# Moving the gate products of a state space mixer two steps forward, and giving the work shared by two engines to VectorE alone around three norms

## The chip, the cores and the metric

The kernel runs on one NeuronCore of one Trainium2 chip. The core has a matrix engine (TensorE, PE in the profile, with PEld for its weight loads), three engines for everything else (VectorE is DVE, ScalarE is ACT, GpSimd is POOL) and a queue that issues transfers (SyncE, SP). Each engine runs its own instructions in the order in which the program lists them, and waits where an operand isn't ready. The metric is the device time of one execution in microseconds (us).

## The reference, cut to what matters

Two layers follow one another on a sequence of 512 tokens with 1024 features. All products are in float32 accuracy.

- First layer: `h = rmsnorm(x)`, a gated delta-rule mixer and a latent attention on `h`, merged by two gates, then `x = x + merged @ w_out`.
- Feed-forward: `h = rmsnorm(x)`, `u = conv(h @ w_up)`, `x = x + (silu(gate_f) * up_f) @ w_down`, and a last `rmsnorm(x)`.
- Second layer: `h = rmsnorm_2(x)` and `proj = h @ w_in`, which is cut into `xbc` (1280 columns), `dt` (16), `z_ssd`, `sc_h`, `sc_b`, `sc_c` and `z_sc` (1024 each).
  - State space part: `xbc` goes through a convolution and SiLU; a chunked scan gives `y_ssd` (16 heads of 64); `yz = y_ssd * silu(z_ssd)`; each of two groups of 512 features is normed by itself.
  - Short convolution: `y_sc = sc_b * conv(sc_c * sc_h) * silu(z_sc)`.
  - `mix = concat(y_ssd, y_sc) @ w_out`, `x = x + rmsnorm(mix)`, and the result is `x + sigmoid(x @ w_ple_gate) * (p @ w_ple_proj)`.

Four norms run over all 1024 features of the residual stream or of `mix`. The change touches the three that stand between two stages of products: the one after `w_out` of the first layer (below: the first norm), the pair after `w_down`, which the kernel computes as one (the second norm), and the one over `mix` (the third norm).

## The kernel before, in words

Activations lie transposed: 128 features on the partitions, the 512 tokens along the row. A product of a 128x128 weight block with a 128x512 tile is three matmuls, because each operand is split into a high part `hi` (rounded to fp32r) and a remainder `lo`: hi by hi, hi by lo and lo by hi. An output tile over 1024 features is 8 blocks, so 24 matmuls of 512 columns. The whole kernel has 1872 such triples.

**Weights.** `order()` (L111) lists the outputs in the order of their products; `pack_weights` lays the blocks out in that order in chunks of 8, and `load_chunk` (L534) streams them. For each chunk `t_chunk` (L557) makes `hi` on ScalarE and `lo` on VectorE or GpSimd; there are two buffers for the raw chunk and three for the split ones.

**Shared work.** `idle` (L431) decides between GpSimd and VectorE for the work that either can do: `lo` of a weight chunk (L570), the multiplication by the norm's scale in `normalised` (L868, tile `xn`), the sum of the squares of some norms (L687), a step of the triangular solve (L1030) and the addition `mix + xr` after the third norm (L1937). It takes the engine that would be free earlier by the program's own clocks, with a bias.

**Planner.** The program is written by generators that are driven by a table of modelled clocks (`Timeline`, L250; `drive`, L467). A generator yields what it waits for; the one whose operand is ready first by the model goes on, the products of the main line when no other is earlier. So the order on each engine's queue is fixed when the program is built, and any change in an engine's modelled load rearranges what comes after it.

**Norms.** `t_rs` (L857) sums the squares as the residual tiles come, transposes and reduces them (`cs`, `ms_a`), takes the inverse root on 128x4 tiles (`rsqrt`, L636: some twelve tiny VectorE instructions), spreads it over the partitions (`bcast`, L665: tile `rs`), and `normalised` multiplies each tile by it and splits it. So that TensorE need not wait, the first three pairs of outputs of the next stage run on the tiles that aren't normed, and are multiplied by `rs` afterwards; `unfold` (L1526) then switches to the normed ones. `t_final` (L1597) does the same for the second norm. The third, `t_post` (L1886) with `t_x2` (L1931), is covered by the eight small `pp` products (`p @ w_ple_proj`), after which the `pg` products need the first normed tile (tile `mix`).

**Second layer.** `block2` (L1890) runs the `xbc` products, and then for each m of 8: the gate product `zs` (its SiLU goes to `zd[m]`), the products `sh`, `sc` (for m of 3 and more; those of the first three ran before), `sb` and `sz`. After the `zs` product of m the generator `t_ssd` of m is spawned (L1779): it loads two rows of 256 KB and two of 128 KB, builds the decay matrices on VectorE, ScalarE and GpSimd, has TensorE compute `y`, adds the skip and multiplies by the gate. At most two of these are at work at a time (`LIMIT`, L222). `t_group` (L1824) norms tiles 0 to 3 and 4 to 7 and splits them into `ym`. The `mix` products follow; each reads 16 activation tiles, `ym` 0 to 7 first and the tiles of the short convolution, 8 to 15, after them. Also in the second layer, `t_dt` (L1643) works out `dt`: a small product, a copy `dtz` on VectorE, and four transposes of it on TensorE, which stand in the middle of the `xbc` products.

Of the kernel before, what the change touches and what calls it, by code (L numbers as in the profile page):

```python
# [37 lines left out]
PAIR_FFN = 3  # L38
FOLD_FFN = 3
FOLD_B2 = 3  # L40
XBC = [8, 9, 0, 1, 2, 3, 4, 5, 6, 7]


# [55 lines left out]
def qr_of(h):  # L99

    return [("qr", 0)] if h == 0 else [("qr", h // 2 + 1)] if h % 2 and h < 7 else []


def order():


    one = lambda keys: [[k] for k in keys]
    kq = lambda h: one([("k", h), ("q", h)])
    vg = lambda h: one([("v", h), ("ga", h)])
    o = [START] + one([("ckv", 0), ("ckv", 1)]) + [FIRST] + one([("q", 1), ("k", 2), ("q", 2)])  # L110
    for item in GDN_ORDER:  # L111
        if item[0] == "kq":
            o += kq(item[1])
        elif item[0] == "vg":
            o += vg(item[1])
        elif item[0] == "low":
            pass
        elif item[0] == "wv":
            o += one([("wv", kt, h) for kt in range(2) for h in range(4 * item[1], 4 * item[1] + 4)])
        elif item[0] in ("bra", "brb", "ya"):  # L120
            o.append([item])
        else:
            h = item[1]
            o += one(qr_of(h) + [("kn", h), ("qn", h)])
    o += [[("yb", 0), ("yb", 1)]] + one([("yb", m) for m in range(2, 8)])
    o += one([("out", m) for m in range(8)])
    pair = lambda f: [("fg", f), ("fu", f)]
    for f in range(12):
        o += [pair(f)] if f < PAIR_FFN else one(pair(f))
    o += one([("fd", 0, m) for m in range(8)])  # L130
    o += one([x for f in range(12, 22) for x in pair(f)])
    o += one([("fd", 1, m) for m in range(8)])
    xbc = [("xbc", m) for m in XBC]
    o += [[("sh", m), ("sc", m)] for m in range(FOLD_B2)] + [["dt2"]] + one(xbc)
    for m in range(8):
        o += one([("zs", m)] + ([("sh", m), ("sc", m)] if m >= FOLD_B2 else []) + [("sb", m), ("sz", m)])
    o += one([("mix", m) for m in range(8)])
    o += one([("pp", m) for m in range(8)])
    o += [[("pg", 0), ("pg", 1), ("pg", 2)]] + one([("pg", m) for m in range(3, 8)])
    return o  # L140
# [92 lines left out]
class Engine:  # L233


    def __init__(self, tl, name, eng):
        self.tl, self.name, self.eng = tl, name, eng
# [157 lines left out]
class Emit:  # L395
# [5 lines left out]
    def __init__(self, ctx, tc, a, out):  # L401
        self.tc, self.a, self.out = tc, a, out
        self.nc = self.tl = Timeline(tc.nc)
        E = ctx.enter_context
        self.const = E(tc.tile_pool(name="const", bufs=1))
        self.wp = E(tc.tile_pool(name="wp", bufs=1))
        self.gp = E(tc.tile_pool(name="gp", bufs=1))
        self.sm = E(tc.tile_pool(name="sm", bufs=1))
        self.ps = E(tc.tile_pool(name="ps", bufs=1, space=PSUM))
        self.dr = E(tc.tile_pool(name="dr", bufs=1, space=DRAM))  # L410
        self.n = 0
        self.nmm = 0
        self.mms = []
        self.held = None
        self.specs = weight_specs()
        self.order = order()
        self.opos = 0
        self.bpos = 0
        self.blocks = {}
        self.his = {}  # L420
        self.nchunk = a["wstream"].shape[0]
        self.loaded = 0
        self.tasks = []
        self.waiting = {}
        self.nspawn = 0
        self.flags = set()
        self.live = []
        self.hold = 1 << 30
        self.using = None

    def idle(self, pool, dve, bias=0):  # L431

        now = self.tl.clk["PE"]
        t = lambda e: max(self.tl.clk[e], now)
        if t("DVE") - now > BACKLOG:
            return self.nc.vector
        return self.nc.gpsimd if t("POOL") + pool <= t("DVE") + dve + bias else self.nc.vector
# [918 lines left out]
    def block1(self):  # L1356
# [155 lines left out]
        def t_out(m, x, ps):  # L1512
            yield [x, ps]
            nc.vector.tensor_tensor(x, x, ps, ALU.add)
            self.xr[m] = x
            self.xh[m] = yield from self.split(x, self.par("norm_ffn_g", m))
# [3 lines left out]
        for m in range(8):  # L1520
            x = self.g(name="xr")
            nc.sync.dma_start(x, self.a["xT"][m])
            ps = yield from self.linear(("out", m), mg)
            self.spawn(t_out(m, x, ps))

    def unfold(self):  # L1526

        self.hold = self.bpos
        yield lambda: hasattr(self, "xn")
        self.hold = 1 << 30  # L1530
        self.xh = self.xn
        self.fold = None
        del self.xn


    def ffn(self):
        nc = self.nc
        hs = [None] * MFF
        self.fold = True

        def t_gate(d, f, ps, fold):
            d["g"] = yield from self.conv(ps, fold, "conv_ffn_w", f, 3, "fg")
            nc.scalar.activation(d["g"], d["g"], AF.Silu)

        def t_up(d, f, ps, fold):
            up = yield from self.conv(ps, fold, "conv_ffn_w", MFF + f, 3, "fu")
            yield lambda: "g" in d
            yield [d["g"]]
            nc.gpsimd.tensor_tensor(up, d["g"], up, ALU.mult)
            hs[f] = yield from self.split(up)  # L1550

        def pair(f):
            d = {}
            keys = ("fg", f), ("fu", f)
            if f < PAIR_FFN:
                pg, pu = yield from self.linears(keys, self.xh)
                self.spawn(t_gate(d, f, pg, self.fold))
            else:
                pg = yield from self.linear(keys[0], self.xh)
                self.spawn(t_gate(d, f, pg, self.fold))  # L1560
                pu = yield from self.linear(keys[1], self.xh)
            self.spawn(t_up(d, f, pu, self.fold))

        def t_down(half, m, ps):
            yield [ps]
            nc.vector.tensor_tensor(self.xr[m], self.xr[m], ps, ALU.add)
            if half:
                yield from self.final_tile(m)

        def down(half):  # L1570
            for m in range(8):
                ps = yield from self.linear(("fd", half, m), hs[11 * half:11 * half + 11] if not half else hs2)
                self.spawn(t_down(half, m, ps))

        for f in range(12):
            if f == FOLD_FFN:
                yield from self.unfold()
            yield from pair(f)
        yield lambda: hs[10] is not None
        yield from down(0)  # L1580
        for f in range(12, 22):
            yield from pair(f)
        yield lambda: hs[21] is not None
        hs2 = hs[11:]
        self.xh = [None] * 8
        del self.rs
        self.spawn(self.t_final())
        yield from down(1)
        del hs, hs2

# [272 lines left out]
    def short_conv(self, m):  # L1863
        nc = self.nc
        if m >= FOLD_B2:
            yield from self.conv_in(m)
# [23 lines left out]
    def block2(self):  # L1890
# [5 lines left out]
        self.sd = {}  # L1896
        for m in range(FOLD_B2):
            yield from self.conv_in(m)
        yield from self.unfold()
        yield from self.dts()  # L1900
        for m in XBC:
            yield from self.xbc([m], self.xs)
# [5 lines left out]
        self.spawn(self.t_group(0))  # L1908
        self.spawn(self.t_group(1))
        zd = {}  # L1910
        for m in range(8):
            ps = yield from self.linear(("zs", m), self.xh)
            self.spawn(self.t_rows(zd, m, ps, AF.Silu, "zs"))
            self.spawn(self.t_ssd(m, zd), "ssd")
            yield from self.short_conv(m)
        mix = [None] * 8
        self.spawn(self.t_post(mix))
        for m in range(8):
            ps = yield from self.linear(("mix", m), self.ym)
            self.spawn(self.t_rows(mix, m, ps, None, "mix"))  # L1920
        ph, pp = [None] * 2, {}
# [107 lines left out]
```

## Time and profile before

| | us |
|---|---|
| median of 3 runs | 1471.09 (1470.6 to 1472.59) |
| the profiled execution | 1473.28 |
| its span, from the first to the last instruction | 1471.5 |
| PE busy in the span | 1444.7 (98%) |
| DVE, ACT, POOL busy | 854.4 (58%), 657.8 (45%), 542.6 (37%) |
| mean granted clock of TensorE, as a share of full speed | 0.993 |

The profiled execution lies 2.19 us above the median of the runs. A busy PE is not yet PE at its peak: a matmul's end is modelled, and at the lower clock the same matmul is busy for longer. So both the idle stretches and the granted clock have to be read.

### The profile page before, as it was taken

How to read it: one execution, taken by the hardware profiler on the slowest of the kernel's cores; microseconds unless marked ns; L12 is line 12 of the kernel's file. 1: busy time of each engine (PE TensorE's matmuls, PEld its weight loads, DVE VectorE, ACT ScalarE, POOL GpSimd, SP SyncE). 2: the span in 40 equal slices, each digit the busy share in tenths (PEclk: the TensorE clock that was granted, in tenths of full speed). 3: DMA queues.
4: the chain of work that ended last, by engine and by line, in shares of the span. 5: the costliest groups of instructions: out<-in, count | busy, mean ns of one | idle time of the engine just before them, and what ended most of it. 6: DMA issues, size and time to landing. Idle time of an engine off the chain costs nothing.

```text
span 1471.5 us, 18957 instructions
## 1 busy us (share of the span) xinstructions
PE 1444.7 (98%) x7084; PEld 1188.1 (81%) x7084; DVE 854.4 (58%) x1701; ACT 657.8 (45%) x1120; POOL 542.6 (37%) x333
## 2 busy tenths in 40 slices
PE   9999999999999999999999999999999999999998
PEld 6788788778878888888888888888787778878877
DVE  7988879687755554367441244446975564360073
ACT  4664335234555663445442244444544544442342
POOL 0333500520334314434554455444024434534421
PEclk9999999999999999999999999999999999999999
DMA  5434313331122224423333223332233433422322
GB/s 190 134 116 143 108 58 85 117 99 32 58 86 74 85 79 129 150 86 101 100 100 101 90 96 100 100 91 88 67 115 113 117 108 102 135 87 86 100 87 100
DMA packets 56891, 147.62 MB, mean 100 GB/s; under 512 B 15008, under 2 KB 15584, under 8 KB 56800
## 3 DMA queue, kind: packets, MB, share of 16 engines
q1 hardware_dynamic: 56800, 146.42, 32.5%
q8 instruction: 55, 0.90, 0.2%
q14 instruction: 36, 0.29, 0.1%
HBM read 139.48 MB, written 5.34 MB: 98 GB/s over the span
## 4 chain that ended last, share of the span: by engine, by line
PE 79%; DVE 13%; POOL 3%; issue 2%; ACT 1%; DMA 1%; SPq 1%; DVEq 0%; POOLq 0%; ACTq 0%
PE mm L244 71%; PE pt L244 8%; DVE lo L244 3%; POOL st L244 1%; POOL sx L244 1%; DVE st L244 1%; DVE sx L244 1%; DVE mix L244 1%; SPq L244 1%; ACT hi L244 0%; DVE Y L244 0%; DVE rq_u L244 0%; DVE qrs L244 0%; DMA x<-xT 0%; DVE v L244 0%
## 5 line engine op out<-in xcount | busy, mean ns | idle before, releaser
L244 PE MATMUL mm<-hi,hi 128*128 128x512 f32 (+2 forms) x1872 | 741.6, 396 | 3.4 <-ACT hi L244 3.4
L244 PE MATMUL mm<-lo,hi 128*128 128x512 f32 (+2 forms) x1872 | 727.0, 388 | 4.5 <-DVE lo L244 4.5
L244 PE MATMUL mm<-hi,lo 128*128 128x512 f32 (+2 forms) x1872 | 726.7, 389 | 2.5 <-DVE lo L244 2.5
L244 POOL TENSOR_TENSOR lo<-raw,hi 128x1024 fp32r<-128x1024 f32 x152 | 365.2, 2403 | 536.4 <-ACT hi L244 509.0
L244 PEld LDWEIGHTS mm<-hi,lo 128*128 128x128 f32 x1872 | 352.6, 188 | 77.9 <-DVE lo L244 4.2
L244 PEld LDWEIGHTS mm<-hi,hi 128*128 128x128 f32 x1872 | 352.9, 188 | 73.8 <-ACT hi L244 4.3
L244 PEld LDWEIGHTS mm<-lo,hi 128*128 128x128 f32 x1872 | 353.3, 189 | 71.4 <-DVE lo L244 5.6
L244 ACT ACTIVATE hi<-raw 128x1024 fp32r<-128x1024 f32 (+1 forms) x230 | 242.5, 1054 | 229.1 <-PE mm L244 164.4
L244 DVE TENSOR_TENSOR lo<-raw,hi 128x1024 fp32r<-128x1024 f32 (+1 forms) x78 | 97.4, 1249 | 3.5 <-ACT hi L244 3.5
L244 DVE TENSOR_TENSOR sq<-sq,sq 128x512 f32<-128x512 f32 x43 | 32.6, 771 | 93.8 <-ACT sq L244 93.6
L244 DVE TENSOR_TENSOR xr<-xr,mm 128x512 f32<-128x512 f32 x24 | 16.5, 687 | 97.5 <-PE mm L244 97.5
L244 DVE TENSOR_TENSOR lo<-fu,hi 128x512 fp32r<-128x512 f32 x22 | 44.5, 2023 | 42.0 <-ACT hi L244 42.0
L244 DVE SCALAR_TENSOR_TENSOR fu<-mm,params,fu 128x510 f32<-128x510 f32 (+1 forms) x38 | 28.5, 749 | 61.6 <-ACT fu L244 60.9
L244 ACT ACT_TABLE_LOAD x39 | 50.0, 1283 | 13.2 <-DVE k L244 6.0
L244 POOL TENSOR_TENSOR q<-q,row 128x512 f32<-128x512 f32 x8 | 10.6, 1319 | 96.6 <-PE pt L244 86.8
L244 POOL TENSOR_TENSOR fu<-fg,fu 128x512 f32<-128x512 f32 x22 | 30.0, 1365 | 42.8 <-DVE fu L244 42.8
L244 DVE TENSOR_TENSOR lo<-scz,hi 128x512 fp32r<-128x512 f32 x8 | 15.8, 1969 | 32.7 <-ACT hi L244 32.7
L244 POOL TENSOR_TENSOR st<-sl,sx 64x247 f32<-64x247 f32 (+15 forms) x31 | 20.8, 672 | 34.3 <-DVE sx L244 25.0
L244 ACT ACTIVATE fg<-fg 128x512 f32<-128x512 f32 x22 | 13.9, 631 | 40.2 <-DVE fg L244 40.2
L244 DVE SCALAR_TENSOR_TENSOR fg<-mm,params,fg 128x510 f32<-128x510 f32 (+1 forms) x38 | 28.2, 743 | 6.2 <-ACT fg L244 5.5
L244 POOL TENSOR_TENSOR xdd<-xd,dd 128x512 f32<-128x512 f32 x8 | 9.4, 1176 | 60.3 <-DVE xd L244 60.2
L244 DVE TENSOR_TENSOR lo<-pt,hi 128x512 fp32r<-128x512 f32 (+3 forms) x32 | 15.6, 487 | 25.9 <-ACT hi L244 25.7
(312 smaller groups left out, 1552.7 us busy)
## 6 DMA issues: line engine op xcount, KB each, us to landing
raw<-wstream SPq DMA_DIRECT2D x228, 512.0 KB, 3.6
row<-grow_d SPq DMA_DIRECT2D x16, 256.0 KB, 4.4
row<-crow_d SPq DMA_DIRECT2D x16, 256.0 KB, 4.7
x<-xT SPq DMA_DIRECT2D x8, 256.0 KB, 5.9
sbd<-gate SPq DMA_DIRECT2D x8, 256.0 KB, 2.1
sb<-sbd SPq DMA_DIRECT2D x8, 256.0 KB, 3.9
xr<-xT SPq DMA_DIRECT2D x8, 256.0 KB, 3.8
Ce<-crow_d SPq DMA_DIRECT2D x16, 128.0 KB, 5.0
```

The source lines that it names most:

```text
L244: return f(*args, **kw)
```

## The change

Two edits. The `zs` product of m, and with it the spawning of `t_ssd` of m, runs two steps ahead: `zs` 0 and 1 come before the first step, and `zs` of m + 2 comes after the products of step m. The weight stream is packed in the same new order.

And a flag `norming` makes `idle` answer VectorE always. It is set when the main line comes to output 6 of the eight `out` products, of the second half of the `fd` (w_down) products and of the `mix` products; `unfold` clears it for the first and the second norm; after the third it stays set to the end. In `normalised` and for the chunks' `lo` parts this means that VectorE alone does that work in these stretches. What GpSimd is given by name, without `idle`, stays with it: the product `rs * rs` and the products `sh * rs2` after the second norm, `fg * fu` of the feed-forward and the gates of the state space part.

```diff
+ZS = 2
...
     o += [[("sh", m), ("sc", m)] for m in range(FOLD_B2)] + [["dt2"]] + one(xbc)
+    o += one([("zs", m) for m in range(ZS)])
     for m in range(8):
-        o += one([("zs", m)] + ([("sh", m), ("sc", m)] if m >= FOLD_B2 else []) + [("sb", m), ("sz", m)])
+        o += one(([("sh", m), ("sc", m)] if m >= FOLD_B2 else []) + [("sb", m), ("sz", m)])
+        if m + ZS < 8:
+            o += one([("zs", m + ZS)])
...
     def idle(self, pool, dve, bias=0):
 
+        if self.norming:
+            return self.nc.vector
         now = self.tl.clk["PE"]
...
         for m in range(8):
             x = self.g(name="xr")
             nc.sync.dma_start(x, self.a["xT"][m])
+            self.norming = m >= 6
             ps = yield from self.linear(("out", m), mg)
...
         self.fold = None
+        self.norming = False
         del self.xn
...
             for m in range(8):
+                self.norming = half == 1 and m >= 6
                 ps = yield from self.linear(("fd", half, m), hs[11 * half:11 * half + 11] if not half else hs2)
...
-        for m in range(8):
+
+        def zs(m):
             ps = yield from self.linear(("zs", m), self.xh)
             self.spawn(self.t_rows(zd, m, ps, AF.Silu, "zs"))
             self.spawn(self.t_ssd(m, zd), "ssd")
+
+        for m in range(ZS):
+            yield from zs(m)
+        for m in range(8):
             yield from self.short_conv(m)
+            if m + ZS < 8:
+                yield from zs(m + ZS)
         mix = [None] * 8
         self.spawn(self.t_post(mix))
         for m in range(8):
+            self.norming = m >= 6
             ps = yield from self.linear(("mix", m), self.ym)
```

## Rows read from the trace of the kernel before

**Rows 1.** The page, part 1: busy us, share and instructions of each engine.
```profile
PE 1444.7 (98%) x7084; PEld 1188.1 (81%) x7084; DVE 854.4 (58%) x1701; ACT 657.8 (45%) x1120; POOL 542.6 (37%) x333
```

**Rows 2.** Busy time by stretch: us; then PE, PEld, DVE, ACT, POOL; clock, DMA.
```profile
650.00:660.00 10.00, 10.00 (x46) 8.29 (x45) 9.96 (x12) 7.66 (x11) 2.65 (x2) 1.00 0.18 60
...
1300.00:1321.00 21.00, 17.41 (x81) 14.09 (x80) 13.95 (x27) 9.38 (x13) 7.50 (x4) 1.00 0.24 75
...
1400.00:1430.00 30.00, 26.37 (x118) 20.88 (x117) 21.34 (x35) 15.08 (x23) 7.80 (x4) 1.00 0.27 81
```

**Rows 3.** The same view, just behind two of the waits.
```profile
1044.30:1050.00 5.70, 5.70 (x21) 4.57 (x22) 5.56 (x10) 2.34 (x4) 0.00 (x0) 0.70 0.02 6
...
1322.00:1326.00 4.00, 4.00 (x12) 3.16 (x11) 1.06 (x2) 0.00 (x0) 0.00 (x0) 0.59 0.24 88
```

**Rows 4.** Timeline, PE: start, us, instruction, idle before; the wait at mix.
```profile
1320.71 0.50 PE L244 MATMUL mm<-lo,hi 128*128 128x512 f32 x1 [3.59 <-DVE lo L244]
```

**Rows 5.** Timeline, ACT and DVE: from the last gate to the splits.
```profile
1288.82 0.60 ACT L244 ACTIVATE zs<-mm 128x512 f32<-128x512 f32 x1 [2.68 <-PE mm L244]
...
1314.10 3.79 DVE L244 SCALAR_TENSOR_TENSOR xbc<-xbc,params,rsg 128x512 f32<-128x512 f32 x4 [4.01 <-ACT rsg L244]
1317.81 4.65 DVE L244 TENSOR_TENSOR lo<-xbc,hi 128x512 fp32r<-128x512 f32 x4
```

**Rows 6.** The page, part 6: a row load of t_ssd, KB and us to landing.
```profile
row<-crow_d SPq DMA_DIRECT2D x16, 256.0 KB, 4.7
```

**Rows 7.** Timeline, PE: the transposes of dtz.
```profile
1044.22 0.43 PE L244 MATMUL pt<-sqc,dtz 32*128 32x32 f32 x4 [2.27 <-DVE dtz L244]
```

**Rows 8.** Timeline, ACT and POOL: around the second norm.
```profile
1011.64 0.59 ACT L244 COPY rs<-pt 128x512 f32<-128x512 f32 x1 [0.23 <-PE pt L244]
...
1011.48 2.40 POOL L244 TENSOR_TENSOR lo<-raw,hi 128x1024 fp32r<-128x1024 f32 x1 [3.04 <-ACT hi L244]
1013.83 1.04 POOL L244 TENSOR_TENSOR rs<-rs 128x512 f32<-128x512 f32 x1
1014.83 1.29 POOL L244 TENSOR_TENSOR xn<-xr,rs 128x512 f32<-128x512 f32 x1
...
1023.49 1.67 POOL L244 TENSOR_TENSOR sh<-sh,rs 128x512 f32<-128x512 f32 x1 [4.41 <-DVE sh L244]
```

**Rows 9.** Timeline, DVE: in the same stretch.
```profile
1016.91 1.01 DVE L244 SCALAR_TENSOR_TENSOR lo<-xn,gg,hi 128x512 fp32r<-128x512 f32 x1 [6.71 <-ACT hi L244]
...
1020.33 0.68 DVE L244 TENSOR_TENSOR xn<-xr,rs 128x512 f32<-128x512 f32 x1
...
1022.07 0.74 DVE L244 SCALAR_TENSOR_TENSOR lo<-xn,gg,hi 128x512 fp32r<-128x512 f32 x1
...
1023.93 1.78 DVE L244 SCALAR_TENSOR_TENSOR lo<-xn,gg,hi 128x512 fp32r<-128x512 f32 x1
...
1043.50 0.67 DVE L244 COPY dtz<-pt 32x512 f32<-32x512 f32 x1
```

**Rows 10.** Timeline, PE, DVE and POOL: the third norm and its waits.
```profile
1421.74 0.49 PE L244 MATMUL mm<-hi,hi 128*128 128x512 f32 x1 [2.70 <-ACT hi L244]
1422.89 0.50 PE L244 MATMUL mm<-lo,hi 128*128 128x512 f32 x1 [0.65 <-DVE lo L244]
...
1410.43 2.20 DVE L244 SCALAR_TENSOR_TENSOR ms_a<-cs,ms_a 128x4 f32<-128x4 f32 x1
...
1417.06 3.36 DVE L244 SCALAR_TENSOR_TENSOR mix<-mix,params,rspost 128x512 f32<-128x512 f32 x3 [2.25 <-ACT rspost L244]
...
1426.55 1.21 DVE L244 TENSOR_TENSOR lo<-raw,hi 128x1024 fp32r<-128x1024 f32 x1
...
1410.21 2.41 POOL L244 TENSOR_TENSOR lo<-raw,hi 128x1024 fp32r<-128x1024 f32 x1 [3.73 <-ACT hi L244]
...
1416.14 2.41 POOL L244 TENSOR_TENSOR lo<-raw,hi 128x1024 fp32r<-128x1024 f32 x1 [3.53 <-ACT hi L244]
```

**Rows 11.** Timeline, POOL: the first norm's scaled tiles.
```profile
647.98 3.00 POOL L244 TENSOR_TENSOR xn<-xr,rs 128x512 f32<-128x512 f32 x2
```

More of the change, by code (lines that the diff above doesn't have):

```diff
@@ L1532, in unfold @@
         self.fold = None
+        self.norming = False
         del self.xn
```

## The prediction, made before the run

> **What bounds the kernel now.** I read the page's busy times first: TensorE is busy for 1444.7 of 1471.5 us [rows 1], so no other engine's load counts by itself; only the 26.8 us in which TensorE stands still can go, and what the stillness does to its clock. The second view is the timeline of TensorE, from which I listed every wait. The first half of the program has many short ones, all ahead of the first line that the change touches. Behind that line there are three places. At the start of the `mix` products TensorE waits 3.59 us for a `lo` of VectorE [rows 4]. Behind the second norm it waits 2.27 us for `dtz`, again VectorE's [rows 7]. After the third norm it waits 2.70 us for the first `hi` and 0.65 us for its `lo` [rows 10]; a last piece of 0.28 us is what is left of the 30.00 - 26.37 = 3.63 us that the busy time by stretch shows there [rows 2]. The first norm has no wait: TensorE is busy for 10.00 of 10 us while VectorE is at 9.96 [rows 2].
>
> The third view is the granted clock. Behind two of the three places it falls: 0.70 of full speed over 5.70 us after the `dtz` wait, and 0.59 over 4.00 us after the `mix` wait [rows 3], which means a part of each stretch at 1.2 instead of 2.4 GHz. The work lost is (1 - 0.70) x 5.70 = 1.71 us and (1 - 0.59) x 4.00 = 1.64 us. The third norm's stretch keeps 1.00 [rows 2]. So the three places cost 3.59 + 1.64 = 5.23, 2.27 + 1.71 = 3.98 and 3.63 us, 12.84 us in all. More than that the change can't give back.
>
> **The gate products, two steps ahead.** Nothing is added: the same eight `zs` products, transfers and vector instructions, in another order. The last gate's SiLU now ends at 1289.4, and the `lo` that TensorE waits for starts at 1317.81, 28 us later [rows 5]: the chain of `t_ssd` 7 and `t_group` 1 lies between, and it starts when `zs` 7 is spawned. In the new order `zs` 7 runs before `sh`, `sc`, `sb` and `sz` of step 6 instead of behind them, so four products of 24 matmuls more follow it. In the stretch from 1300 to 1321, 17.41 us hold 81 matmuls, of which the tiny ones are few [rows 2]; at 17.41 / 81 = 0.215 us each, four products are at least 96 x 0.215 = 20.6 us. The splits come some 20 us earlier against TensorE, and a wait of 3.59 us goes whole. What is late next is the last tile of the short convolution, which is `ym` 15, the sixteenth tile that the first `mix` product reads; before, its split stood behind the four splits of rows 5, which end at 1322.46, and TensorE didn't wait for it. Without the four in front it is earlier. With the wait the fall of the clock goes: -5.2 us, with 0 as the other end if another wait takes its place.
>
> The moved steps issue their transfers earlier too: two rows of 256 KB (4.7 us to landing [rows 6]) and two of half that for each `t_ssd`, on SP's queue among the weight loads. `t_ssd` 0 and 1 now go one behind the other, which puts about 1.5 MB in a row at the first step. The weights are loaded ahead by two chunks, and TensorE's 3.59 us at 1320.71 is its only wait from 1300 to 1321 [rows 2, 4], with such loads shortly before. I take nothing for it; uncovered, the second group would hold up the weights by about one landing, 4.7 us, once. GpSimd's products for `t_ssd` move with it, and it is busy for 7.50 of 21 us there [rows 2]: nothing.
>
> **VectorE alone, second norm.** Before, `rs` is there at 12.23 (all of these are 1000 and more). GpSimd is in the middle of a weight's `lo` until 13.88, multiplies `rs * rs` until 14.87 and makes the first `xn` until 16.12 [rows 8]. VectorE has been idle for 6.71 us when it starts its first split at 16.91 [rows 9], and from there on it works to `dtz` at 43.50, 2.27 us too late. After the change the `lo` is VectorE's, in its idle time, so `rs * rs` can start at 12.3, and VectorE makes the first `xn` at 12.3 or, if GpSimd's product is first, at 13.3. It then has 16.91 - 13.3 = 3.6 to 16.91 - 12.3 = 4.6 us for work that stood in the full stretch. Against that it gets three `xn` of 0.68 us, 2.04 us; and GpSimd's three `xn` no longer hold it up. A like hold-up shows at 23.93, where a split takes 1.78 us instead of 0.74 while GpSimd works [rows 8, 9], so 1.04 us for one; I count 0 to 3 x 1.04 = 3.1 us back for the three. So `dtz` comes earlier by 3.6 - 2.0 + 0 = 1.6 to 4.6 - 2.0 + 3.1 = 5.7 us, middle 3.6, and 2.27 are wanted. I take the middle: the wait goes, and the fall of the clock with it: -4.0 us. The lower end leaves 0.7 us of wait.
>
> The row of 1023.93 shows a split of VectorE that starts inside GpSimd's `sh` product (1023.49 to 1025.16) and ends 1.04 us late [rows 8, 9]. The Trainium skill (SBUF — State Buffer, "SBUF: two separate sides") says more sharply that the two engines share a port pair under an exclusive lock, and that whichever starts first keeps it for its whole instruction while the other fully blocks. By this rule the change also loses: the products that GpSimd keeps (`rs * rs`, `sh * rs2`) now meet the `xn` and splits that VectorE starts at once. By the rule the sum would keep a wait at `dtz`; it is the first rival.
>
> **Third norm.** VectorE's `ms_a` on 128x4 takes 2.20 us and ends at 1412.63, with GpSimd's `lo` that ends at 1412.62 [rows 10]. With the `lo` on VectorE, 1.21 us [rows 10], the chain gains 2.20 - 1.21 = 1.0 us if that `lo` stands in front of it, and close to 2.2 if not. The same holds for the three scalings that start at 1417.06, while GpSimd is in a `lo` until 1418.55: up to 1.49 us lost there, against 1.21 for the `lo` on VectorE, so 0.3 to 1.5. Together 1.3 to 3.7, of which 3.63 can be had. Behind the first tile VectorE is nearly full, and another weight's `lo` (1.21 us) there lengthens it. I take 2.0, half way between 1.3 and 3.7 less some of that. The flag stays set to the end; the three chunks that GpSimd splits in the last 40 us then go to a VectorE that only finishes outputs, which I cost at 0, and at 1.21 us if the last of them is late.
>
> **First norm.** VectorE gets two `xn` (3.00 us on GpSimd [rows 11], 2 x 0.68 here) and one more weight's `lo`, 1.36 + 1.21 = 2.6 us, into a stretch where it is at 9.96 of 10 [rows 2], and is rid of what GpSimd's products cost it. TensorE has no wait there to win. I take 0; the ends are 0 and 2.6 us lost.
>
> **A term for the new plan.** All that follows the first flag is planned anew. Small pieces such as the 0.65 and 0.28 us of the third norm come and go; I add 1.0 us, with 0 and 2 as its ends.
>
> **The sum.** -5.2 - 4.0 - 2.0 + 1.0 = -10.2 us. The profiled execution took 1473.28 us, its span of 1471.5 and 1.8 around it; the same execution after the change would take 1463.1. It lies 2.19 us above the median of 1471.09; carried to the median, 1460.9 us.
>
> **The rivals.**
> 1. The second norm's wait stays, because GpSimd's remaining products block VectorE in place of the ones taken away. For it: the 1.04 us of rows 9, and 1.04 + 1.67 us of GpSimd's fixed products [rows 8], which can eat 2.7 of the 4.6 us. Against it: GpSimd has much less to do there. Then -5.2 - 1.3 + 1.0 = -5.5: 1465.6 us.
> 2. Another wait takes the place of the one at `mix`: the short convolution's last split, or the weights held up by the row loads. For it: VectorE's splits stood full up to 1322.46. Against it: 20 us of lead. The place keeps its 5.23 us, the norms give 4.0 + 2.0 less 1.0: -5.0, 1466.1 us.
> 3. Slower: VectorE becomes the bound around the norms. Its queue is in order, so each split that it is given ahead of a chain delays the chain whole. That decides once VectorE was full without GpSimd's interference: no hold-up comes back, and the moved work is added, 2.6 us at the first norm, 2.04 + 1.21 = 3.3 at the second, 2 x 1.21 = 2.4 at the third, and one fall of the clock, 1.7: +10.0, against -5.2 at `mix`: 1475.9 us. For it: 9.96 of 10 at the first norm. Against it: 6.71 us of idleness at the second, and `ms_a` held up for 2.2 us.
> 4. The change doesn't move the time: VectorE had most of this work already, and the new plan loses elsewhere what `mix` gives. 1471 us, give or take 2.9.
>
> **How the numbers follow.** Forecast 0.52, rivals in order 0.20, 0.10, 0.07 and 0.11. A measurement of this kernel can tell about 0.2%, 2.9 us, from no change, so the forecast and rivals 1 and 2 count as faster: 0.82; rival 4 as the same: 0.11; rival 3 as slower: 0.07. The likeliest's own range is 1458.3 (all 12.84 us) to 1464.0 (the low ends of the norms: 5.2 + 1.6 + 1.3 - 1.0 = 7.1 us). The range for 8 in 10 reaches over rivals 1 and 2 to 1468.0 and starts at 1458.0.
>
> **What would show it.** Right: at the first `mix` product no wait on VectorE and a clock of 1.00; the last `y` of `t_ssd` 7 before step 6 ends; the first `xn` on VectorE within 2 us of `rs`, and `dtz` before its transposes' turn; `ms_a` of the third norm at about 0.2 us and less than 2 us of waiting before the first `pg` product. Wrong: a new wait of TensorE of over 2 us in the stretches from `xbc` to `mix`, a fall of the clock that isn't there now, weights' `lo` as the releaser of TensorE around a norm, or a wait on a transfer behind the row loads.

## The result, and the profile after

| | before | after |
|---|---|---|
| median of 8 runs, us | 1473.01 (1470.6 to 1477.48) | 1465.61 (1464.52 to 1467.11) |
| the profiled execution, us | 1473.28 | 1467.05 |
| its span, us | 1471.5 | 1465.3 |

The ratio is 0.9945, with a 95% interval from 0.9936 to 0.9954: 8.1 us faster (6.8 to 9.4), where 10.2 were forecast; the medians of the table are 7.4 us apart. With more runs the median of before came out 1.9 us higher than the one that the forecast started from; the predicted 1460.9 is 4.7 us below the measured 1465.61, which lies inside the range of 1458.0 to 1468.0, but above the likeliest's own range, which ends at 1464.0.

The page of the kernel after, part 1 (the answer to [rows 1]): GpSimd does 48 us less, VectorE 14 us more.

```profile
PE 1442.8 (98%) x7084; PEld 1185.9 (81%) x7084; DVE 868.4 (59%) x1723; ACT 656.5 (45%) x1120; POOL 495.0 (34%) x311
```

Busy time by stretch, after (the answer to [rows 2, 3]; the clock is the first number behind POOL's):

```profile
650.00:660.00 10.00, 10.00 (x46) 8.29 (x45) 9.93 (x14) 6.99 (x9) 1.98 (x1) 1.00 0.22 62
...
1040.00:1050.00 10.00, 9.09 (x43) 7.08 (x41) 9.41 (x25) 6.50 (x9) 0.00 (x0) 1.00 0.10 40
1294.00:1315.00 21.00, 21.00 (x94) 17.38 (x93) 11.46 (x12) 8.84 (x13) 9.03 (x5) 1.00 0.27 82
1315.00:1325.00 10.00, 10.00 (x46) 8.28 (x45) 2.47 (x1) 2.64 (x3) 6.05 (x3) 1.00 0.29 103
1395.00:1425.00 30.00, 28.17 (x124) 21.95 (x123) 20.49 (x40) 15.66 (x24) 0.00 (x0) 1.00 0.27 87
```

The start of the `mix` products has no wait any more (21.00 of 21.00), the clock stays at 1.00 there and behind `dtz`, and the third norm waits for 2.11 us in place of 3.63: 1.83 in the 30 us shown and 0.28 right behind them, at 1427.47. These are TensorE's waits behind the first changed line, all but one of 0.28 us (timeline of PE, after):

```profile
1034.59 0.39 PE L248 MATMUL pt<-hi,dtw 128*32 128x512 f32 x1 [0.60 <-DVE dtw L248]
1042.10 0.43 PE L248 MATMUL pt<-sqc,dtz 32*128 32x32 f32 x4 [0.91 <-DVE dtz L248]
1051.02 0.63 PE L248 MATMUL pt<-gg,sqc 128*128 128x64 f32 x4 [0.79 <-DVE gg L248]
1124.10 0.65 PE L248 MATMUL pt<-row,xd 128*64 128x128 f32 x6 [0.65 <-DVE row L248]
1413.99 0.50 PE L248 MATMUL mm<-hi,hi 128*128 128x512 f32 x1 [0.38 <-ACT hi L248]
1415.26 0.50 PE L248 MATMUL mm<-lo,hi 128*128 128x512 f32 x1 [0.76 <-DVE lo L248]
1418.33 0.50 PE L248 MATMUL mm<-lo,hi 128*128 128x512 f32 x1 [0.65 <-DVE lo L248]
```

A stop costs more than the idle time in its brackets. The matmul before the one of 1413.99 starts 0.77 us ahead of it, where the brackets say 0.38; without a wait the starts are 0.23 us apart.

```profile
1413.00 0.39 PE L248 MATMUL mm<-lo,hi 128*128 128x512 f32 x1
1413.22 0.39 PE L248 MATMUL mm<-hi,lo 128*128 128x512 f32 x1
```

To say where the time went I lined the two executions up by their work. The kernels have 5472 product matmuls of 512 columns, in the same number per stage, so the start of the n-th one can be compared; the times are read from the timeline of PE.

```
product matmul (from 0)         0    1920     3720     4080     4920     5280     5471
start before, us             5.77  597.77  1007.60  1106.17  1330.38  1412.96  1461.26
start after, us              5.79  598.29  1008.12  1105.46  1324.98  1407.53  1455.03
change of the stretch              +0.50     0.00    -1.23    -4.69    -0.03    -0.80
```

The first stretch, to 1920, is the same program in both: +0.50 is what two executions differ by. The first norm lies in the second (0.00). A, from 3720 to 4080, holds the second norm: -1.23. B, to 4920, holds the gates, the state space part and the start of `mix`: -4.69. C, from 5280 to the end, holds the third norm: -0.80. From 1920 to the end that is -6.75 us.

### The profile page after: what moved, and what is told of

Same layout as the page of the kernel before. It is cut to its first block, busy times and chain, and to the rows that moved or that the text cites. A ratio compares the mean times of both kernels' runs of the same rounds, so it can differ in the third digit from the quotient of the medians.

```text
span 1465.3 us, 18961 instructions
## 1 busy us (share of the span) xinstructions
PE 1442.8 (98%) x7084; PEld 1185.9 (81%) x7084; DVE 868.4 (59%) x1723; ACT 656.5 (45%) x1120; POOL 495.0 (34%) x311
## 4 chain that ended last, share of the span: by engine, by line
PE 79%; DVE 11%; POOL 3%; issue 2%; DMA 2%; ACT 2%; SPq 1%; DVEq 0%; POOLq 0%; ACTq 0%
PE mm L248 72%; PE pt L248 8%; DVE lo L248 2%; POOL st L248 1%; POOL sx L248 1%; DVE st L248 1%; SPq L248 1%; ACT hi L248 1%; DVE mix L248 1%; DVE row L248 1%; DVE sx L248 1%; DVE Y L248 0%; DVE qrs L248 0%; DMA sl<-ldram 0%; DVE xr L248 0%
## 5 line engine op out<-in xcount | busy, mean ns | idle before, releaser
L248 POOL TENSOR_TENSOR lo<-raw,hi 128x1024 fp32r<-128x1024 f32 x135 | 325.3, 2410 | 466.9 <-ACT hi L248 401.3
L248 DVE TENSOR_TENSOR lo<-raw,hi 128x1024 fp32r<-128x1024 f32 (+1 forms) x95 | 120.1, 1265 | 22.5 <-ACT hi L248 22.4
L248 DVE TENSOR_SCALAR row<-row,cmp 128x128 f32<-128x128 f32 x64 | 27.8, 504 | 0.0
```

The source lines that it names most:

```text
L248: return f(*args, **kw)
```

## The experiments

All stand against the kernel before, run on the same chip; A, B, C and the last column are the changes of the stretches as in the table above, from one profiled execution of each.

```
                    ratio to before  interval         A      B      C   from 1920 on
changed kernel               0.9945  0.9936-0.9954  -1.23  -4.69  -0.80  -6.75
e1_zs_only                   0.9960  0.9944-0.9975  -0.03  -4.68  +1.80  -2.93
e2_norm_only                 0.9980  0.9969-0.9992  -1.18  +1.20  -0.76  -0.78
e3_no_pool_second            0.9929  0.9913-0.9946  -3.99  -4.69  -0.76  -9.46
e4_xr_late                   0.9941  0.9926-0.9956  -3.15  -4.70  -0.79  -8.68
e5_rspost_dve                0.9952  0.9940-0.9965  -1.18  -4.70  -0.76  -6.68
e6_lo_only                   0.9958  0.9945-0.9970  -1.00  -4.69  -0.80  -6.53
e7_xn_only                   0.9969  0.9959-0.9979  -1.46  -4.66  +0.97  -5.14
e8_zs3                       0.9959  0.9945-0.9973  -1.24  -3.99  -0.79  -6.05
e9_hold_lo                   0.9958  0.9946-0.9971  -1.22  -4.70  -0.72  -6.68
e10_no_pool_hold             0.9940  0.9928-0.9953  -4.01  -4.70  -0.76  -9.49
e11_mix_alone                0.9974  0.9965-0.9984  +0.02  -3.40  +1.02  -2.36
e12_all                      0.9938  0.9926-0.9951  -3.93  -4.68  -0.74  -9.38
```

### Each edit alone

e1_zs_only, against the changed kernel:

```diff
-        if self.norming:
-            return self.nc.vector
```

> The gate products run ahead as in the changed kernel, but the flag does nothing: VectorE and GpSimd share as before. Theory A (the two edits act at separate places and add up): the wait of 3.59 us at the first mix product and the fall of the clock behind it go, 5.2 us, and a new wait of 0.65 us in the first t_ssd stays as in the changed kernel; the 2.27 us at dtz with its fall of the clock, and the 3.6 us at the third norm stay: 4.0 to 5.5 us faster than before, 1 to 3 us slower than the changed kernel. Theory B (the wait at mix went because VectorE and GpSimd no longer meet in that stretch, or because the whole plan came out otherwise): the mix wait stays at 2 us or more, and the kernel is within 1.5 us of before.

e2_norm_only, against the changed kernel (with 1 the order is that of before):

```diff
-ZS = 2
+ZS = 1
```

> The flag acts at all three norms, the gate products stand where they stood before. Theory A (the edits act at separate places): the mix wait of about 3.6 us and the fall of the clock behind it stay; dtz about 0.9 us without a fall of the clock, third norm about 2.1 us in all: 1.5 to 3.5 us faster than before. Theory B (one plan, the flag did most of it): 5 us or more faster than before, with the mix wait gone.

Measured: 5.9 us and 2.9 us faster than before by the ratios, 8.8 us together, against 8.1 for both edits at once. e1's 5.9 is a little more than theory A's 4.0 to 5.5; the interval, 3.7 to 8.3, reaches over it. The places are separate. e1 keeps the waits of both norms and loses the one at `mix`; e2 the other way round (timelines of PE, e1 and then e2):

```profile
1044.68 0.51 PE L248 MATMUL pt<-sqc,dtz 32*128 32x32 f32 x4 [2.26 <-DVE dtz L248]
1417.45 0.80 PE L248 MATMUL mm<-hi,hi 128*128 128x512 f32 x1 [2.70 <-ACT hi L248]
```

```profile
1041.97 0.43 PE L248 MATMUL pt<-sqc,dtz 32*128 32x32 f32 x4 [0.91 <-DVE dtz L248]
...
1319.92 0.79 PE L248 MATMUL mm<-lo,hi 128*128 128x512 f32 x1 [3.59 <-DVE lo L248]
```

Theory A holds for the places. What neither theory had is e1's +1.80 in C: its waits there are those of before, but behind them the clock falls (0.79 and 0.80 us for a matmul), which in the profiled execution of before it didn't. e2's +1.20 in B is of the same kind: the same wait of 3.59 us, and a fall twice as long behind it (last section).

### What is left of the second norm's wait

e3_no_pool_second, against the changed kernel:

```diff
-        nc.gpsimd.tensor_tensor(self.rs2, self.rs, self.rs, ALU.mult)
+        nc.scalar.activation(self.rs2, self.rs, AF.Square)
...
-                nc.gpsimd.tensor_tensor(d["h"], d["h"], self.rs2, ALU.mult)
+                nc.vector.tensor_tensor(d["h"], d["h"], self.rs2, ALU.mult)
```

> The changed kernel, but GpSimd has no work left around the second norm: rs squared is made on ScalarE, and the three products of sh by it on VectorE. Theory A (GpSimd's remaining products hold VectorE up there: four hold-ups of 0.8 to 1.1 us, 4.0 us in all, show in the changed kernel's trace, and 3 x 0.68 = 2.0 us of work come to VectorE): dtz comes about 2 us earlier, its wait of 0.91 us goes, 0.5 to 1.5 us faster than the changed kernel. Theory B (VectorE's queue order decides: five scalings of the residual stand in front of dtz): the hold-ups go, the scalings are planned earlier or later with them, the dtz wait stays between 0.5 and 2 us, and the time stays within 0.5 us of the changed kernel.

e4_xr_late, against the changed kernel:

```diff
         self.xr = self.x1
+        yield self.flag("dt")
         for m in range(8):
             nc.vector.scalar_tensor_tensor(self.xr[m], ...
```

> The changed kernel, but the eight scalings of the residual tiles after the second norm, which nobody needs before the third norm, are only issued once the work for dt is done; the work itself is the same. Theory B (VectorE's queue order decides what is left of the dtz wait): 5 x 0.66 = 3.3 us no longer stand in front of dtz, the waits of 0.91 us at dtz and perhaps 0.79 us at gg go: 0.8 to 2.0 us faster than the changed kernel. Theory A (GpSimd's hold-ups are what delays dtz): the dtz wait stays above 0.5 us, within 0.5 us of the changed kernel.

Both theories hold; either edit does it, and e3 gives more than the 0.5 to 1.5 us that its theory A expected. First the changed kernel's own second norm (timelines of DVE and then POOL, after; they answer to [rows 8, 9]):

```profile
1011.69 2.14 DVE L248 TENSOR_TENSOR xn<-xr,rs 128x512 f32<-128x512 f32 x2 [1.43 <-ACT rs L248]
1013.75 2.31 DVE L248 TENSOR_TENSOR lo<-raw,hi 128x1024 fp32r<-128x1024 f32 x1
...
1024.23 1.78 DVE L248 SCALAR_TENSOR_TENSOR lo<-xn,gg,hi 128x512 fp32r<-128x512 f32 x1
...
1035.83 2.32 DVE L248 TENSOR_TENSOR lo<-raw,hi 128x1024 fp32r<-128x1024 f32 x1
1038.07 3.39 DVE L248 SCALAR_TENSOR_TENSOR xr<-xr,params,rs 128x512 f32<-128x512 f32 x5
1041.38 0.67 DVE L248 COPY dtz<-pt 32x512 f32<-32x512 f32 x1
...
1011.74 1.55 POOL L248 TENSOR_TENSOR rs<-rs 128x512 f32<-128x512 f32 x1 [30.88 <-ACT rs L248]
1013.36 1.62 POOL L248 TENSOR_TENSOR sh<-sh,rs 128x512 f32<-128x512 f32 x1
...
1035.33 1.73 POOL L248 TENSOR_TENSOR sh<-sh,rs 128x512 f32<-128x512 f32 x1 [9.87 <-DVE sh L248]
```

VectorE starts 5.2 us earlier than before (1011.69 against 1016.91), but `dtz` only 2.1 us (1041.38 against 1043.50); measured from product 3720, which this execution reaches 0.52 us later, 5.7 and 2.6 us. In between lie the hold-ups by GpSimd's remaining products: two `xn` in 2.14 us where e3 needs 1.29, two weights' `lo` of 2.31 and 2.32 us instead of 1.22, and the split of 1.78 us instead of 0.74, 4.1 us in all. The kernel before had as much of it: the first split of 1.01 us and the split of 1.78 us [rows 9], and (timeline of DVE, before)

```profile
1018.16 2.25 DVE L244 SCALAR_TENSOR_TENSOR ysc<-sh,params,ysc 128x510 f32<-128x510 f32 x2 [0.24 <-ACT ysc L244]
...
1025.63 2.31 DVE L244 TENSOR_TENSOR lo<-raw,hi 128x1024 fp32r<-128x1024 f32 x1
...
1036.57 1.78 DVE L244 SCALAR_TENSOR_TENSOR xr<-xr,params,rs 128x512 f32<-128x512 f32 x1
```

where the same instructions elsewhere take 1.52, 1.22 and 0.74 us: 4.2 us in all. And five scalings of the residual, 3.39 us that nobody wants before the third norm, stand right in front of `dtz`.

The 2.6 us would still have covered the wait of 2.27. But the new plan also gave the instructions that wait an earlier turn on TensorE. Counted from the timelines of PE:

```
                                              before   after      e3      e4
product matmuls ahead of the product by dtw     3834    3828    3825    3822
product matmuls ahead of dtz's transposes       3849    3840    3840    3828
product matmuls ahead of gg's first matmul      3894    3873    3876    3861
dtz copied, us from the start of product 3720  36.57   33.93   31.66   30.11
```

Nine product matmuls are 9 x 0.228 = 2.05 us, so 2.27 + 2.05 = 4.32 us were wanted and 2.64 came. The 1.68 us that lack are the waits of 0.60 us at `dtw` and 0.91 at `dtz`, and what the first stop costs beyond its brackets. The wait of 0.79 us at `gg` is new because its turn comes 21 matmuls earlier. No run keeps the turns of before, so what that alone would give was not measured.

Without GpSimd (e3) the same row reads

```profile
1012.18 1.29 DVE L248 TENSOR_TENSOR xn<-xr,rs 128x512 f32<-128x512 f32 x2 [1.42 <-ACT rs L248]
...
1039.59 0.67 DVE L248 COPY dtz<-pt 32x512 f32<-32x512 f32 x1
```

with all the scalings still ahead of `dtz`; `dtz` comes 2.27 us earlier than in the changed kernel at the same turn, no wait is left in A, and A is 2.8 us shorter. With the scalings held back (e4) `dtz` comes at

```profile
1036.14 1.54 DVE L248 SCALAR_TENSOR_TENSOR ysc<-sh,params,ysc 128x510 f32<-128x510 f32 x2 [2.17 <-ACT ysc L248]
1037.59 0.67 DVE L248 COPY dtz<-pt 32x512 f32<-32x512 f32 x1
```

and 0.64 us at `dtw` are the only wait left. In e4 the last of the four hold-ups is gone too (GpSimd's third `sh` product meets no weight's `lo`), so e4 doesn't stand for the scalings alone. I had expected theory A and theory B to exclude each other: VectorE was short of some 2 us, and either source gives them.

e6_lo_only and e7_xn_only split the flag: the weights' `lo` alone, or the scaled tiles alone. `share` makes `idle` decide as before.

```diff
-        if self.norming:
+        if self.norming and not share:
# e6
-            if self.idle(1300, 700, POOL_BIAS if keep else 0) is nc.gpsimd:
+            if self.idle(1300, 700, POOL_BIAS if keep else 0, True) is nc.gpsimd:
# e7
-        lo_eng = self.idle(2500, 1150, 0 if c < 8 else POOL_BIAS) if c else nc.vector
+        lo_eng = self.idle(2500, 1150, 0 if c < 8 else POOL_BIAS, True) if c else nc.vector
```

> The changed kernel, but the flag moves only the weights' lo to VectorE; the scaling of the tiles after the first and the second norm is shared as before. Theory E (the weights' lo held the start of the second norm up, GpSimd being in the middle of one when the scale came): dtz waits 1.5 us or less, no fall of the clock behind it, within 0.7 us of the changed kernel. Theory F (the scaled tiles on GpSimd held VectorE up): the dtz wait is back at 2 us or more, with a fall of the clock, 1.2 to 3 us slower than the changed kernel.

> The changed kernel, but the flag moves only the scaling of the tiles after the first and the second norm to VectorE; the weights' lo are shared as before everywhere. Theory E: the dtz wait is at 2 us or more, with a fall of the clock behind it, and the third norm loses its gain of 0.8 us too: 2 to 3.5 us slower than the changed kernel. Theory F: the dtz wait stays at about 0.9 us; only the third norm's 0.8 us are lost.

The `dtz` wait, e6 and then e7:

```profile
1041.35 0.43 PE L248 MATMUL pt<-sqc,dtz 32*128 32x32 f32 x4 [0.83 <-DVE dtz L248]
```

```profile
1041.23 0.43 PE L248 MATMUL pt<-sqc,dtz 32*128 32x32 f32 x4 [1.00 <-DVE dtz L248]
```

Neither theory alone: half of the flag is as good as the whole in A (-1.00 and -1.46 against -1.23), and the two halves don't add. e7's waits in C are those of before, with a fall of the clock behind them.

### The wait at mix

e8_zs3, against the changed kernel:

```diff
-ZS = 2
+ZS = 3
```

> The changed kernel with the gate products one step more ahead (three before the first step). If 20 us of lead were more than the 3.6 us that were wanted, as predicted, nothing is left to win at mix: within 0.5 us of the changed kernel there, no wait at mix in both. If the wait of 0.65 us in the first t_ssd came from two of them at work at once beside the gates, it stays or grows to 1 us or more; a rival, that the row loads of the earlier t_ssd hold up the weights, would show a wait on a transfer or on a weight's split there and 2 us or more lost.

No wait at `mix`, as in the changed kernel; B is 0.7 us longer, with the 0.66 us in the first `t_ssd` and 0.22 us more in the next. That is a little more than the 0.5 us that were expected. No wait on a transfer. With `ZS = 1` the order is that of before, so the change moves `zs` 7 forward past one step's four products, as the prediction reckoned, and not past two steps as its title says; that one step is enough.

e11_mix_alone, against the kernel before: the flag is set from the last step's `sh` to the first `mix` product, and nowhere else.

```diff
         for m in range(8):
+            self.norming = m == 7
             yield from self.short_conv(m)
...
         for m in range(8):
+            self.norming = m < 1
             ps = yield from self.linear(("mix", m), self.ym)
```

> The kernel before, with its order of the gate products, and with the flag at no norm, but from the last step of the gate products to the first mix product: VectorE alone takes the weights' lo there. Theory A (the mix wait is a matter of the chain's late start): the chain from the last gate to the splits stays 25 us or longer, the mix wait stays above 1.5 us; GpSimd's lo holds the first split up by 1.9 us in the trace of before, and the scalings by about 1 us, which is all that can go; 0 to 3 us faster than before. Theory B (the two engines' meeting makes the wait): the wait falls below 0.7 us, 3.5 us or more faster than before.

Between the two, and nearer to theory B (timelines of PE and of DVE, e11):

```profile
1317.41 0.50 PE L248 MATMUL mm<-lo,hi 128*128 128x512 f32 x1 [0.28 <-DVE lo L248]
1319.76 0.50 PE L248 MATMUL mm<-lo,hi 128*128 128x512 f32 x1 [0.70 <-DVE lo L248]
...
1312.10 2.08 DVE L248 SCALAR_TENSOR_TENSOR xbc<-xbc,params,rsg 128x512 f32<-128x512 f32 x3 [1.43 <-ACT rsg L248]
1314.10 0.69 DVE L248 TENSOR_TENSOR lo<-xbc,hi 128x512 fp32r<-128x512 f32 x1
```

The gates stand where they stood, and 3.59 us of wait become 0.98, without a fall of the clock; 0.36 us more go at the group norm. The first split runs 0.69 us, while in before four splits took 4.65 us [rows 5]: the first of them 2.84 us, beside a weight's `lo` of GpSimd (before, duration min/median/max in ns, and timeline of POOL).

```profile
L244 DVE TENSOR_TENSOR lo<-xbc,hi x4: 677/678/2842, 1317.8 to 1321.8; 128x512 fp32r<-128x512 f32 x4
...
1317.57 2.53 POOL L244 TENSOR_TENSOR lo<-raw,hi 128x1024 fp32r<-128x1024 f32 x1 [0.23 <-ACT hi L244]
```

In the changed kernel the meeting is still there and the chain from the last gate to the splits still takes 28 us, but it starts 21.7 us earlier (timelines of ACT and DVE, after):

```profile
1267.16 0.60 ACT L248 ACTIVATE zs<-mm 128x512 f32<-128x512 f32 x1 [2.68 <-PE mm L248]
...
1296.15 4.09 DVE L248 TENSOR_TENSOR lo<-xbc,hi 128x512 fp32r<-128x512 f32 x3
```

So either remedy works: an earlier start of the chain takes the wait away with the meeting left in, and ending the meeting takes most of it away with the late start left in. The Trainium skill (SBUF — State Buffer, "SBUF: two separate sides") says that a VectorE instruction with two inputs in SBUF and a GpSimd instruction that reads SBUF share a port pair, which the first holds for its whole instruction while the other fully blocks. The rows of e3 and e11 agree; a meeting cost VectorE 0.85 to 1.1 us at the second norm, and 2.84 - 0.68 = 2.2 us at this split.

### What is left of the third norm's waits

e5_rspost_dve, against the changed kernel (`bcast` gets an argument for the engine):

```diff
-        self.rsp = yield from self.bcast(r, "rspost")
+        self.rsp = yield from self.bcast(r, "rspost", self.nc.vector)
```

> The changed kernel, but the third norm's scale is copied from PSUM by VectorE instead of ScalarE. In the changed kernel the inverse root is there at 1408.4, and VectorE starts its first scaling at 1411.8: ScalarE has a copy and a weight's hi in front of the scale's copy, and VectorE a weight's lo (1.2 us) in front of the scaling. Theory C (what the third norm gained was given back in ScalarE's queue): the scaling starts about 1 us earlier after the root, the waits at the third norm fall from 2.1 to about 1.2 us: about 0.9 us faster than the changed kernel. Theory D (VectorE's own load, two instructions more in a full stretch, sets the third norm's waits): the waits stay at 1.8 us or more, within 0.4 us of the changed kernel.

e9_hold_lo: the edit of e5, and

```diff
         yield [hi]
+        yield lambda: not self.third
         lo = part("lo")
...
-        r = yield from self.meanrs(mix, D, apart=True)
+        a = yield from self.meansq(mix, D, apart=True)
+        self.third = True
+        r = yield from self.rsqrt(a, NC)
...
+            self.third = False
             x2[m] = yield from self.split(t)
```

> The changed kernel with the third norm's scale copied by VectorE, and besides no weight's lo is issued from the mean square of the third norm on until its first tile is scaled and added. Theory C2 (two weights' lo of 1.2 us each, in front of the root and in front of the first scaling in VectorE's queue, set what is left of the third norm's waits): the first scaling starts 2 us or more earlier, the waits there fall from 2.1 us to 1.0 or less, 0.8 to 1.8 us faster than the changed kernel. Theory D (VectorE's load as a whole sets them: the two lo come right behind and delay the second and third tile as much): the hi wait goes, the lo waits grow, the sum stays above 1.7 us, within 0.5 us of the changed kernel.

Theory D, both times: C stays at -0.76 and -0.72. In e5 the scale is there earlier, but the weight's `lo` stands before the first scaling (timeline of DVE, e5):

```profile
1408.25 0.69 DVE L248 COPY rspost<-pt 128x512 f32<-128x512 f32 x1 [1.11 <-PE pt L248]
1409.39 1.23 DVE L248 TENSOR_TENSOR lo<-raw,hi 128x1024 fp32r<-128x1024 f32 x1 [0.45 <-ACT hi L248]
1410.53 0.75 DVE L248 SCALAR_TENSOR_TENSOR mix<-mix,params,rspost 128x512 f32<-128x512 f32 x1
```

In e9 the two held weights come right behind the first tile and delay its own split (timelines of DVE and PE, e9):

```profile
1411.91 0.69 DVE L248 TENSOR_TENSOR mix<-mix,xr 128x512 f32<-128x512 f32 x1
1412.52 2.35 DVE L248 TENSOR_TENSOR lo<-raw,hi 128x1024 fp32r<-128x1024 f32 x2
...
1416.12 0.68 DVE L248 TENSOR_TENSOR lo<-mix,hi 128x512 fp32r<-128x512 f32 x1
...
1416.85 0.50 PE L248 MATMUL mm<-lo,hi 128*128 128x512 f32 x1 [1.34 <-DVE lo L248]
```

The wait for `hi` is gone, the one for `lo` has grown from 0.76 to 1.34. Three orders of nearly the same work on VectorE (e5 and e9 add one copy of 0.69 us) cost the same. That VectorE's load sets these waits is argued from this; no run takes load away from it there.

### A better kernel

e10_no_pool_hold has the edits of e3 and e9, e12_all those and e4's.

> The edits of the last experiment and those that take GpSimd's work from around the second norm, together, as a candidate for a better kernel. If the places are independent: the second norm gives 2.8 us more than in the changed kernel, the third what the last experiment gives; 3 to 4.5 us faster than the changed kernel, 0.75 to 0.85% faster than before. If the plan interferes: less than 2 us.

> The candidate, and the scalings of the residual tiles held back until dt is done as well. With GpSimd out of the second norm no wait is left at dtz, dtw or gg, so nothing is expected of it there: within 0.5 us of the candidate. If the scalings then fall into the xbc products and delay their convolutions, a wait of 0.5 us or more shows between 1045 and 1110.

By the work from 1920 on, both are as good as e3 alone (-9.49, -9.38 and -9.46), since e9 gives nothing and e4 nothing more once GpSimd is out; the 3 to 4.5 us expected of e10 over the changed kernel came out as 2.7. e3 is the simplest: 0.9929 (0.9913 to 0.9946) of before. Against the changed kernel that is 2.7 us by the trace; by the times the intervals overlap.

## Why the prediction came out as it did

- **`mix`, -5.2: right in size and mechanism.** The wait and the fall of the clock went, because the chain starts 21.7 us earlier. B shows -4.69, and the new wait of 0.65 us in the first `t_ssd`, where `row` isn't ready, accounts for the rest (e1 has it, e2 with the old order not). Row loads and weights on SP's queue cost nothing. The cause of the wait was told too simply: the 28 us of chain were not all needed work, and e11 takes most of the wait away without moving the chain's start.
- **Second norm, -4.0: the step that failed.** "2.27 are wanted. I take the middle: the wait goes." 1.23 us came of it. The fall of the clock went, but a wait of 0.91 us stayed and 0.60 and 0.79 us appeared at `dtw` and `gg`. `dtz` came 2.64 us earlier, inside the 1.6 to 5.7 that were reckoned; what was wrong is that its turn on TensorE was taken as fixed, while the new plan moved it forward by nine products, 2.05 us. And it could have come earlier: GpSimd's remaining products held VectorE up, as the first rival said (e3), and the plan put the scalings of the residual in front of `dtz`, eight of them instead of five (e4). The hold-ups that I had credited to the change as 0 to 3.1 us didn't fall: 4.2 us before, 4.1 after. The first two come from `rs * rs` and the `sh` product behind it, which now meet VectorE's first `xn` and `lo`; the other two from the later `sh` products.
- **Third norm, -2.0: mis-sized, -0.80.** `ms_a` takes 0.16 us instead of 2.20, as stated; but a weight's `lo` stands inside the root and another before the first scaling (timeline of DVE, after):

```profile
1405.00 0.16 DVE L248 SCALAR_TENSOR_TENSOR ms_a<-cs,ms_a 128x4 f32<-128x4 f32 x1
...
1405.35 1.22 DVE L248 TENSOR_TENSOR lo<-raw,hi 128x1024 fp32r<-128x1024 f32 x1
...
1410.66 1.23 DVE L248 TENSOR_TENSOR lo<-raw,hi 128x1024 fp32r<-128x1024 f32 x1 [2.25 <-ACT hi L248]
```

  Behind the first tile two other orders gave no more (e5, e9). The idle time fell by 1.52 us, from 3.63 to 2.11, and the stretch by only 0.80: four stops have taken the place of three, and each costs more than its idle time. The lower end, 1.3 us less "some of that", was the place to stay.
- **First norm, 0: right,** 0.00 with VectorE at 9.93 of 10.
- **The new plan, +1.0: too small, if taken by itself.** The waits that are new come to 0.65 + 0.60 + 0.79 = 2.04 us, the upper end. They are already in the figures of `mix` and of the second norm above, so they don't count twice.
- **The rivals.** That the measured 1465.61 is the 1465.6 of rival 1 is luck: rival 1 is 5.5 us below a median of 1471.09 that came out at 1473.01 with more runs, and the change gave 8.1. Of its mechanism, GpSimd's remaining products are shown by e3; the earlier turn and the scalings it doesn't have. Rival 3's 1475.9 is refuted; weights' splits that VectorE was given did stand in front of the chain at the third norm, but cost less than was won there.
- **Not in the sum:** the third norm's 3.63 us of wait could also drop the clock. In the profiled execution of before it didn't; in the three others without the flag at that norm it did (next section). The trace's -6.75 us can't show this, and the times may. The mean granted clocks point that way without showing the place: 0.992 over 18 executions of before (e1's record) and 0.996 over the 8 of after, against 0.993 and 0.995 in the two profiled ones. That it makes up the difference to 8.1 us was not shown.

## What to carry to other kernels

Work that two engines can share isn't free on either: a meeting cost VectorE 0.85 to 2.2 us here, so moving an operation from GpSimd pays with the meetings it ends, and only if those that stay don't just move to a new place. Time won at the start of an in-order queue goes to whatever the planner puts next into it; before counting it for the instruction that is waited for, look for filler in front of that instruction, and hold the filler back. Look at the other side too: a planner that expects a result earlier may also give the instruction that waits for it an earlier turn, and then the wait stays. And where a wait ends with a chain, ask first which of the chain's instructions run longer than they do elsewhere.

## What the runs showed of the hardware that I had not expected

A wait of 2.7 us may or may not bring the clock down to 1.2 GHz, and the fall varies in length, so nearly the same waits cost a different time from one execution to the next. At the third norm, with the same 2.70 and then 0.35 to 0.65 us of waiting, before keeps 1.00 [rows 2], e1 has 0.62 over 9 us, e7 0.72 over 6 and e11 0.76 over 7 (busy time by stretch, each in its own kernel):

```profile
1417.00:1426.00 9.00, 8.20 (x23) 6.20 (x24) 9.00 (x15) 4.54 (x7) 0.00 (x0) 0.62 0.15 49
```

```profile
1414.00:1420.00 6.00, 5.35 (x16) 4.09 (x16) 6.00 (x10) 2.63 (x4) 0.00 (x0) 0.72 0.00 0
```

```profile
1417.00:1424.00 7.00, 6.20 (x19) 4.72 (x20) 7.00 (x12) 3.19 (x6) 0.00 (x0) 0.76 0.00 1
```

By (1 - clock) x length that is 3.4, 1.7 and 1.7 us of work; C, which holds it, grew by 1.80, 0.97 and 1.02 us. None of the ten kernels with the flag at the third norm fell there. In e2 the unchanged wait of 3.59 us at `mix` cost 0.43 x 8 = 3.4 us, twice as much as in before:

```profile
1319.00:1327.00 8.00, 7.08 (x19) 5.62 (x20) 3.28 (x5) 0.30 (x1) 0.32 (x1) 0.57 0.23 68
```

The first 1920 product matmuls are the same program in all fourteen kernels, and the next one starts between 595.93 us (e7) and 601.09 us (e10): a spread of 5 us that no edit made. It is why the stretches are compared here and not only the times.
